# Three couples in the first chunk of a Strassen matmul, with VectorE's order and the results' sources moved

## The chip, the cores and the metric

The kernel runs on one core of one Trainium2 chip. Its time is device time in microseconds, the median over several executions. A profile is one execution in which a hardware profiler also records the instructions; its times are counted from the start of the span, which is a little shorter than the device time of that execution. A "slot" below is the time of sixteen 512-column matmuls on TensorE, the unit in which the kernel plans.

## The reference

```python
a: (4096, 4096) float32, b: (4096, 4096) float32, bias: (4096,) float32
out = np.tanh(np.matmul(a, b) + bias)
```

## The kernel before

The product is made in float16 with Strassen's scheme in Winograd's form: a block of the output is cut into four quarters and computed with seven products m1 to m7 instead of eight.

**Chunks and items.** The 4096 output columns are four chunks of 1024. In a chunk, 16 pairs of 128-row tiles are worked off. An *item* is such a pair with the chunk's columns: 256 rows by 1024 columns, seven products of 16 matmuls each (128x128 weights from a, 512 columns from b, contraction 2048). `PRODUCTS` names for each product its left operand (a quarter or a sum of quarters of a: a11, a12, a21, a22, s1, s2, s5, s6, s7) and its right operand (b11, b22, or sums d1, d3, d4, e6, e7 of quarters of b, kept in SBUF for the whole chunk). In the first chunk, three pairs are done in the opening in the plain way (lines 1459 and before), items 0 to 10 are single pairs, and items 11 and 12 do two pairs half and half, where chunks meet.

**Slots.** Everything is written out by hand in slots: `at_slot(slot, f, ...)` hangs work on a slot, and the loop at the end of the kernel goes through the slots, first runs the work hung there, then issues the products due, then the groups of the couples. An item n has the slots from 7n on; its products stand at positions 0 (m2), 2 (m5), 4 (m3), 5 (m1), 6 (m4), 8 (m6), 10 (m7), so that two items interleave. Each engine executes its queue strictly in the order in which this loop writes it: an instruction that waits holds up everything behind it on that engine.

**What is prepared for an item.** `prepare(n)` hangs up the loads of a (`load_nat`, GpSimd's queue, float32 to float16, sixteen of 128 KB per item, into tiles called `nat`), the turns (`turn`: VectorE transposes `nat` tiles into the quarters, line 281), the sums s1 to s7 (`asum`, VectorE, line 155), and `keep`, which stores the quarters in DRAM for the later chunks (SyncE's queue, line 311). The sums are made in place: s2 and then s6 over a21, s5 and then s7 over a12. The pool `wide` has eight tiles; an item's `nat` data take four of them. A load into such a tile waits until the turns that read it are through, and the quarters have two buffers each, so a turn waits until TensorE has read the same quarter of two items before (for a21 that is m6, which reads s6).

**After a product.** `after` takes sums and results. m2 and m5 share a bank: VectorE makes two sums with the bias from the bank after m2 (into the d bank and into `s`), and m5 then accumulates onto it, so it has to wait for both. After m3 ScalarE copies the bank to `cs`, after m4 to `ds`; `result` lets ScalarE make the tanh into a tile `o` of the pool `outs` (three tiles), and `store` writes it out (SyncE's queue, line 504). m1's sum writes into m3's bank, which becomes the bank of m6.

**Couples.** In two places of the first chunk two items are a *couple* (`ones`, set by `ONE_BASE` and `ONES`; the second item of a couple is in `behind_one`): their m3 are computed together with one more level of Strassen, seven products of eight matmuls at 256 columns instead of 32 at 512. The groups are issued at positions 4 (`group0`), 6 (`group1`), 8 (`single` 7 and 3 with m1, then `single` 4). They need four sums of a11 of both items (`left`, tiles `h`, two tiles of `wide` from `new_lefts` on until `end_ones`), three sums of d3 in tiles `one` and a fourth in place of a quarter of d3; that quarter is stored to DRAM before (`move`, SyncE) and brought back after the last couple (`end_ones`, GpSimd). `group1` and `twice_four` add an intermediate `x` to halves of the two items' banks; the last group writes into a half that the second of these adds reads.

In the trace, line 489 is `product`, line 794 is `multiply` (the groups of a couple), line 155 is every tensor_tensor of VectorE, line 281 the transposes, line 514 `result`, line 253 and 261 the loads, line 643 `move`. In row names a number behind a tile's name tells buffers apart.

Of the kernel before, what the change touches and what calls it, by code (L numbers as in the profile page):

```python
# [47 lines left out]

LEAD = 3
BEHIND = {"m7": 9}, {"m4": 3}  # L50
ONE_BASE, ONES = 6, 2
ONE_AT = {"m1": 8, "m4": 5, "m6": 10}
ONE_FROM = SLOTS * ONE_BASE - 1
FIRST = {0: 6, 2: 0, 4: 4, 5: 5, 6: 2, 8: 8, 10: 10}
# [70 lines left out]
def kernel(  # L125
# [391 lines left out]
    def after(n, s, what, st):  # L517
        c, pairs, part, _ = items[n]
        pair = pairs[s]
        first, last = part in (None, 0), part in (None, 1)  # L520
        if what == "m2":
            add21 = bias_bc[:, :NB] if first else asides[pair][0]
            add12 = bias_bc[:, NB:] if first else asides[pair][1]
            st["d"] = bank(n, s, "d")
            if n in second:
                st["ds"] = temps.tile([P, NB], fp32, name="ds", tag="ds")
                tt(st["ds"], st["z"], add21, ADD)
            else:
                tt(st["d"], st["z"], add21, ADD)
            st["s"] = temps.tile([P, NB], fp32, name="s", tag="sc")  # L530
            tt(st["s"], st["z"], add12, SUB)
        elif what == "m5":
            st["c"] = bank(n, s, "c")
            if n in twos or n in ones or n in behind_one:
                tt(st["s"], st["z"], st["s"], SUB)
                if n in second or n in behind_one:
                    twice_after(n, "m3")
            else:
                tt(st["c"], st["z"], st["s"], SUB)
        elif what == "m3":  # L540
            if last:
                st["cs"] = temps.tile([P, NB], fp32, name="cs", tag="sc")
                nc.scalar.copy(st["cs"], st["c"])
                if not first:
                    tt(st["cs"], st["cs"], asides[pair][2], ADD)
                result(st["c"], pair, 0, c, 1)
            else:
                asides[pair] = [
                    tl[:, i]
                    for tl in (wide.tile([P, 2, NB], fp32, name="aside", tag="wide") for _ in range(2))  # L550
                    for i in range(2)
                ]
                nc.scalar.copy(asides[pair][1], st["c"])
        elif what == "m1":
            if last:
                st["v"] = bank(n, s, "v")
                if n in partner or n in ones:
                    twice_four(n, "m3", 2)
                if n < len(items) - 1:
                    tt(st["v"], st["cs"], st["z"], SUB)  # L560
                else:
                    st["w"] = bank(n - 1, s, "z")
                    for to, half in ((st["v"], LAST[0]), (st["w"], LAST[1])):
                        tt(to[:, half], st["cs"][:, half], st["z"][:, half], SUB)
            else:
                st["v"] = bank(n, s, "v")
                nc.scalar.activation(st["v"], st["z"], COPY, scale=-1.0)
        elif what == "m4":
            if last:
                st["ds"] = temps.tile([P, NB], fp32, name="ds", tag="ds")  # L570
                nc.scalar.copy(st["ds"], st["d"])
                if not first:
                    tt(st["ds"], st["ds"], asides[pair][3], ADD)
                result(st["d"], pair, 1, c, 0)
            else:
                nc.scalar.copy(asides[pair][0], st["d"])
        elif what == "m6":
            if last:
                result(st["v"], pair, 1, c, 1)
            else:  # L580
                nc.scalar.copy(asides[pair][2], st["v"])
        else:
            if last:
                if n in twos and n + 2 < len(items) and not again(n + 2) and not natural(n + 2):
                    fetch(n + 2, "a12")
                o = new_out()
                tt(o, st["ds"], st["z"], SUB)
                nc.scalar.activation(o, o, TANH)
                store(o, pair, 0, c, 0)
            else:  # L590
                nc.scalar.activation(asides[pair][3], st["z"], COPY, scale=-1.0)
# [710 lines left out]
    def lead_after(n, what, st):  # L1302
        c, (pair,), part, _ = items[n]
        if what == "m2":
            st["c"] = bank(n, 0, "c")
            tt(st["c"], bias_bc[:, NB:], st["z"], SUB)
            if n:
                set_aside(st)
        elif what == "m3":
            st["cs"] = temps.tile([P, NB], fp32, name="cs", tag="sc")  # L1310
            nc.scalar.copy(st["cs"], st["c"])
            result(st["d"], pair, 1, c, 0)
        elif what == "m1":
            st["v"] = st["c"]
            tt(st["v"], st["cs"], st["w"], SUB)
        elif what == "m5":
            o = new_out()
            tt(o, st["cs"], st["z"], ADD)
            nc.scalar.activation(o, o, TANH)
            store(o, pair, 0, c, 1)  # L1320
            tt(st["ds"], st["ds"], st["z"], SUB)
        elif what == "m6":
            result(st["v"], pair, 1, c, 1)
        elif what == "m7":
            o = new_out()
            tt(o, st["ds"], st["w"], SUB)
            nc.scalar.activation(o, o, TANH)
            store(o, pair, 0, c, 0)

# [6 lines left out]
    def prepare(n):  # L1336
# [5 lines left out]
        elif natural(n):  # L1342
            loads = {0: (-5, -4), 1: (4, 5), 2: (6, 7)}.get(n, (s0 - 7, s0 - 4))
            for r in (1, 0):
                at_slot(loads[r if n in behind_one else 1 - r], load_nat, n, r)
                if n == 1 and r:
                    at_slot(loads[0], store_ends, "A")
            turns = {
# [4 lines left out]
            }.get(n, [(i, (s0 + x, s0 + y)) for i, (x, y) in {  # L1353
                "a22": (0, 0), "a21": (2, 2), "a11": (3, 4), "a12": (5, 5)
            }.items()])
            if n in behind_one:
                turns = [(i, (s0 + x, s0 + y)) for i, (x, y) in (
                    ("a11", (0, 1)), ("a22", (2, 2)), ("a21", (3, 3)), ("a12", (4, 5)),
                )]
            if n == 4 and n not in behind_one:  # L1360
                turns[0] = "a22", (s0 + 1, s0 + 1)
            if n - 3 in fours and part is not None:
                turns[0] = "a22", (s0 + 1, s0 + 2)
            if n - 2 in fours:
                turns = [("a22", (3, 3)), ("a21", (4, 4)), ("a11", (5, 8)), ("a12", (6, 8))]
                turns = [(i, (s0 + x, s0 + y)) for i, (x, y) in turns]
            for name, at in turns:
                at_slot(at[0], turn, n, name, 0)
            for name, at in turns:
                at_slot(at[1], turn, n, name, 1)  # L1370
                if n == 0 and name == "a22":
                    at_slot(-1, asum, n, "s2", 0)
                if name in ("a11", "a22") and not stays(n):
                    at_slot({0: {'a22': -1, 'a11': 5}, 1: {'a22': 12, 'a11': 15}, 2: {'a22': 17, 'a11': 18}}.get(n, {}).get(name, at[1]), keep, n, name)
        else:
            behind = n - 2 in partner
            for name, at in (
                ("a22", 1 if behind else 0), ("a21", 1),
                ("a11", -1 if n in second else 0 if behind else 2), ("a12", 4),
            ):  # L1380
                if part == 1 and n - 2 in fours and name != "a12":
                    continue
                if name == "a12" and n - 2 not in twos and n > LEAD + 1 and n - 2 not in fours:
                    early_fetch.add(n)
                elif name != "a12" or n - 2 not in twos:
                    at_slot(s0 + at, fetch, n, name)
# [17 lines left out]
        if natural(n) and n - 2 in fours:  # L1404
            sums_at["s2"], sums_at["s5"] = 5, 8
        if n in ones:
            sums_at.update(s1=14, s6=15, s7=15)
        if n - 2 in twos and n not in twos and part is None:
            sums_at["s5"] = 8
        for name, at in sums_at.items():  # L1410
# [386 lines left out]
```

## Time and profile before

| | |
|---|---|
| runs shown | 1502.38, 1502.63, 1508.91 us |
| median | 1502.63 us |
| profiled execution | 1501.84 us, span 1499.9 us |
| TensorE clock granted, mean | 0.999 |
| TensorE busy | 1492.3 us of the span |
| VectorE, ScalarE, GpSimd busy | 1226.1, 404.1, 528.5 us |
| first chunk's items | from about 90 us to about 400 us |
| couples of the first chunk | m3's first group at 244.65 and at 292.85 us |

The profile's rows are to be read so: start in us, length in us, engine, line, operation, written tile <- read tiles, shapes, count; in brackets the idle time of the engine before the row and what ended it. Lists of waits give engine and line that waited, what it waited for, total us, number of times, longest. PE is TensorE, DVE VectorE, ACT ScalarE, POOL GpSimd, SPq SyncE's DMA queue. Rows that begin with a stretch such as 260.00:270.00 give busy us (and instructions) of TensorE's matmuls, its weight loads, VectorE, ScalarE and GpSimd, then the granted clock, the busy share of the DMA engines and GB/s. The length of a matmul row is modelled, so the pace is read from the starts.

### The profile page before, as it was taken

How to read it: one execution, taken by the hardware profiler on the slowest of the kernel's cores; microseconds unless marked ns; L12 is line 12 of the kernel's file. 1: busy time of each engine (PE TensorE's matmuls, PEld its weight loads, DVE VectorE, ACT ScalarE, POOL GpSimd, SP SyncE). 2: the span in 40 equal slices, each digit the busy share in tenths (PEclk: the TensorE clock that was granted, in tenths of full speed). 3: DMA queues.
4: the chain of work that ended last, by engine and by line, in shares of the span. 5: the costliest groups of instructions: out<-in, count | busy, mean ns of one | idle time of the engine just before them, and what ended most of it. 6: DMA issues, size and time to landing. Idle time of an engine off the chain costs nothing.

```text
span 1499.9 us, 25071 instructions
## 1 busy us (share of the span) xinstructions
PE 1492.3 (99%) x9509; PEld 927.9 (62%) x9509; DVE 1226.1 (82%) x1742; ACT 404.1 (27%) x915; POOL 528.5 (35%) x925
## 2 busy tenths in 40 slices
PE   9999999999999999999999999999999999999998
PEld 4444445444445788864444578888644468888886
DVE  6788979887787888967888788889658869888887
ACT  4431111111222233321122223333222222333332
POOL 8775454354523111245751321111434121111112
PEclk9999999999999999999999999999999999999999
DMA  9999999799999799889999988998998687888895
GB/s 186 184 244 266 298 268 271 188 256 204 185 343 306 258 326 342 314 308 260 191 286 323 288 287 311 329 341 311 318 280 213 221 286 269 299 321 300 324 339 184
DMA packets 211132, 413.51 MB, mean 276 GB/s; under 512 B 26178, under 2 KB 102466, under 8 KB 211012
## 3 DMA queue, kind: packets, MB, share of 16 engines
q0 software_dynamic: 124992, 220.00, 59.2%
q1 hardware_dynamic: 85348, 191.53, 36.4%
q8 instruction: 74, 1.21, 0.3%
q10 hardware_dynamic: 672, 0.39, 0.1%
q14 instruction: 46, 0.38, 0.1%
HBM read 352.33 MB, written 138.94 MB: 328 GB/s over the span
## 4 chain that ended last, share of the span: by engine, by line
PE 93%; DMA 4%; DVE 2%; issue 0%; POOL 0%; ACT 0%; DVEq 0%; POOLq 0%
PE ps L489 42%; PE ps L794 37%; PE ps L858 9%; PE ps L1459 6%; DMA nat<-in_a_dram 3%; DVE a L281 1%; DVE a L155 1%; DMA coarse<-in_a_dram 0%; DVE s L155 0%; DVE h L155 0%; POOL nat L261 0%; DVE ps L155 0%; POOL nat L253 0%; PE warm L1519 0%; PE spread L452 0%
## 5 line engine op out<-in xcount | busy, mean ns | idle before, releaser
L489 PEld LDWEIGHTS <-a 128*128 128x128 f16 x2592 | 253.0, 98 | 303.2 <-issue 0.9
L794 PEld LDWEIGHTS <-h 128*128 128x128 f16 x3008 | 293.6, 98 | 37.6
L730 POOL DMA_DIRECT2D form<-form_m x196 | 103.9, 530 | 537.0 <-PE ps L794 485.2
L794 PEld LDWEIGHTS <-a 128*128 128x128 f16 x2256 | 220.1, 98 | 36.5 <-issue 1.4
L489 PE MATMUL ps<-b,a 128*128 128x512 f16 x868 | 198.2, 379 | 0.4 <-DVE s L155 0.4
L489 PE MATMUL ps<-d,a 128*128 128x512 f16 x800 | 180.3, 379 | 0.0
L281 DVE STREAM_TRANSPOSE a<-nat 128x1024 f16<-128x1024 f16 (+3 forms) x178 | 155.8, 917 | 19.9 <-PE ps L489 15.3
L155 DVE TENSOR_TENSOR a<-a,a 128x2048 f16<-128x2048 f16 (+1 forms) x135 | 162.5, 1206 | 0.2
L489 PE MATMUL ps<-e,a 128*128 128x512 f16 x700 | 158.7, 379 | 0.0
L794 PE MATMUL ps<-form,h 128*128 128x256 f16 x1136 | 144.7, 273 | 0.0
L155 DVE TENSOR_TENSOR h<-a,h 128x1024 f16<-128x1024 f16 x188 | 127.9, 687 | 15.8 <-PE ps L794 15.7
L391 POOL DMA_DIRECT2D b<-in_b_dram x208 | 112.0, 543 | 74.7 <-PE ps L489 33.4
L794 PE MATMUL ps<-form,a 128*128 128x256 f16 x896 | 111.5, 273 | 0.2
L253 POOL DMA_DIRECT2D nat<-in_a_dram x144 | 76.5, 535 | 93.3 <-DMA nat<-in_a_dram 48.0
L858 PE MATMUL ps<-d,a 128*128 128x512 f16 x480 | 108.2, 379 | 0.0
L489 PEld LDWEIGHTS <-s 128*128 128x128 f16 x624 | 60.9, 98 | 72.4
L880 ACT CAST ps<-zeros 128x256 f32<-128x256 f16 x196 | 70.1, 380 | 127.7 <-DVE s L155 68.9
L858 PEld LDWEIGHTS <-a 128*128 128x128 f16 x608 | 59.4, 98 | 65.9
L489 PE MATMUL ps<-d,s 128*128 128x512 f16 x432 | 97.6, 379 | 0.0
L155 DVE TENSOR_TENSOR ds<-ds,ps 128x512 f32<-128x512 f32 (+1 forms) x126 | 83.5, 674 | 9.2 <-PE ps L858 8.3
L155 DVE TENSOR_TENSOR ps<-ps,x 128x256 f32<-128x256 f32 x100 | 43.0, 430 | 47.4 <-PE ps L794 37.2
L794 PE MATMUL ps<-d,a 128*128 128x256 f16 x608 | 78.8, 273 | 0.0
(173 smaller groups left out, 1950.3 us busy)
## 6 DMA issues: line engine op xcount, KB each, us to landing
form<-form_m POOLq DMA_DIRECT2D x196, 512.0 KB, 7.2
a<-scratch SPq DMA_DIRECT2D x148, 512.0 KB, 7.3
out_dram<-o SPq DMA_DIRECT2D x186, 256.0 KB, 6.0
nat<-in_a_dram POOLq DMA_DIRECT2D x256, 128.0 KB, 7.8
scratch<-a SPq DMA_DIRECT2D x48, 512.0 KB, 8.3
b<-in_b_dram POOLq DMA_DIRECT2D x176, 128.0 KB, 5.6
form_m<-stage POOLq DMA_DIRECT2D x18, 512.0 KB, 6.5
scratch<-a SPq DMA_DIRECT2D x32, 256.0 KB, 8.1
```

Of the source, the lines that this page charges most:

```text
L155: nc.vector.tensor_tensor(out=out_, in0=in0, in1=in1, op=op)
L253: nc.gpsimd.dma_start(out=tl[ds(q * QP, QP), :, :], in_=src.rearrange("(mb p) k -> p mb k", p=QP),)
L281: nc.vector.transpose(dst[:, ds(b0 * tb, n * tb), :].rearrange("P (b t) (mb p) -> P mb b t p", t=tb, p=QP), src[:, :, ds(b0, n), :].rearra ...
L391: nc.gpsimd.dma_start(out=dst[ds(q * QP, QP), ds(t, nt)], in_=src)
L489: nc.tensor.matmul(st[where], at, bt, start=(what == "m2" or n < LEAD and what == "m1") and i == 0, stop=i == len(ts_) - 1, skip_group_che ...
L730: nc.gpsimd.dma_start(out=rights[what, name], in_=forms[what, name])
L794: nc.tensor.matmul(to, at, bt, start=False, stop=t == TP - 1, skip_group_check=True)
L858: nc.tensor.matmul(to[:, half], at[:, t // TB, t % TB], bop[right, t // TB][:, t % TB, half], start=anew and t == 0, stop=t == T - 1, skip ...
L880: nc.scalar.copy(bank(n, 0, where)[:, HALF[half]], zeros)
L1459: nc.tensor.matmul(mb[m % 4, j], aq[m, kt // T][:, kt % T, :], right(kt, j), start=fresh and kt == k0, stop=stop and kt == k1 - 1, skip_gr ...
```

## The change

Four things change, all in the first chunk except where `after` serves a few single items of later chunks:

- `ONE_BASE, ONES = 5, 3`: the couples are items (5, 6), (7, 8), (9, 10) instead of (6, 7), (8, 9). The sums of d3 are made seven slots earlier, its quarter is stored seven slots earlier (slot 20 instead of 27), and brought back seven slots later (72 instead of 65).
- s6 and s7 of a couple's first item are hung on the slot after the one that holds the couple's third step (16 instead of 15, counted from seven slots before the item).
- The turn of a22 of every item of the first chunk from item 4 on, other than the second of a couple, stands a slot later, behind the sums of m2. Before, only item 4 had this.
- The tanh of m3 and m4 reads ScalarE's copy instead of the bank, and m7's sum and tanh are made in place in `ds` instead of a tile of `outs`.

```diff
-ONE_BASE, ONES = 6, 2
+ONE_BASE, ONES = 5, 3
...
-                result(st["c"], pair, 0, c, 1)
+                result(st["cs"] if first else st["c"], pair, 0, c, 1)
...
-                result(st["d"], pair, 1, c, 0)
+                result(st["ds"] if first else st["d"], pair, 1, c, 0)
...
-                o = new_out()
+                o = st["ds"] if c == 0 and part is None else new_out()
                 tt(o, st["ds"], st["z"], SUB)
...
-            o = new_out()
-            tt(o, st["ds"], st["w"], SUB)
+            o = st["ds"]
+            tt(o, o, st["w"], SUB)
...
-            if n == 4 and n not in behind_one:
+            if n >= 4 and items[n][0] == 0 and n not in behind_one:
                 turns[0] = "a22", (s0 + 1, s0 + 1)
...
         if n in ones:
-            sums_at.update(s1=14, s6=15, s7=15)
+            sums_at.update(s1=14, s6=16, s7=16)
```

What that makes of VectorE's queue in the first couple, from its second-last step on. Before (items 6 and 7; a22_2254 is a22 of item 8, the sums over a21_1919 and a12_2004 are s6 and s7 of item 6, x_2250 the intermediate):

```order
L155 TENSOR_TENSOR a11_1942<-a22_1865,a11_1942 128x2048
L281 STREAM_TRANSPOSE a22_2254<-nat_2056 128x2x16x32
L281 STREAM_TRANSPOSE a22_2254<-nat_2061 128x2x16x32
L155 TENSOR_TENSOR ps_0_247<-ps_7_254,bias_bc_109 128x512
L155 TENSOR_TENSOR s_2286<-ps_7_254,bias_bc_109 128x512
L155 TENSOR_TENSOR a21_1919<-a21_1919,a11_1942 128x2048
L155 TENSOR_TENSOR a12_2004<-a11_1942,a12_2004 128x2048
L155 TENSOR_TENSOR ps_2_249<-ps_2_249,x_2250 128x256
L155 TENSOR_TENSOR s_2090<-ps_5_252,s_2090 128x512
L155 TENSOR_TENSOR ps_5_252<-s_2090,ps_4_251 128x512
```

After, VectorE at the same place of its first couple (items 5 and 6; a22_2091 is a22 of item 7, the sums over a21_1736 and a12_1817 are s6 and s7 of item 5):

```order
L155 TENSOR_TENSOR a11_1759<-a22_1711,a11_1759 128x2048
L155 TENSOR_TENSOR ps_6_253<-ps_4_251,bias_bc_109 128x512
L155 TENSOR_TENSOR s_2089<-ps_4_251,bias_bc_109 128x512
L281 STREAM_TRANSPOSE a22_2091<-nat_1867 128x2x16x32
L281 STREAM_TRANSPOSE a22_2091<-nat_1872 128x2x16x32
L155 TENSOR_TENSOR ps_5_252<-ps_5_252,x_2056 128x256
L155 TENSOR_TENSOR s_1899<-ps_2_249,s_1899 128x512
L155 TENSOR_TENSOR ps_2_249<-s_1899,ps_7_254 128x512
L155 TENSOR_TENSOR a21_1736<-a21_1736,a11_1759 128x2048
L155 TENSOR_TENSOR a12_1817<-a11_1759,a12_1817 128x2048
```

The two sums of m2 (those that read `bias_bc`) now stand ahead of the turn of a22, and s6 and s7 behind the add of `x` and the two sums of m3 and m1.

The second place is where the item after the last couple begins, again on VectorE. Before (a22_2864 is a22 of item 11; the sums with `bias_bc` follow m2 of item 10):

```order
L155 TENSOR_TENSOR ps_2_249<-s_2683,ps_7_254 128x512
L155 TENSOR_TENSOR a12_2583<-a11_2470,a12_2583 128x2048
L155 TENSOR_TENSOR a12_2820<-a12_2820,a11_2763 128x2048
L281 STREAM_TRANSPOSE a22_2864<-nat_2656 128x4x8x32
L281 STREAM_TRANSPOSE a22_2864<-nat_2661 128x4x8x32
L155 TENSOR_TENSOR ps_6_253<-ps_4_251,bias_bc_109 128x512
L155 TENSOR_TENSOR s_2894<-ps_4_251,bias_bc_109 128x512
L155 TENSOR_TENSOR s1_2915<-a22_2652,a11_2763 128x2048
```

After (the item that follows the last couple is item 11, whose two pairs need two such sums each; a22_3104 is a22 of item 12):

```order
L155 TENSOR_TENSOR ps_5_252<-s_2882,ps_4_251 128x512
L155 TENSOR_TENSOR a12_2786<-a11_2674,a12_2786 128x2048
L155 TENSOR_TENSOR a12_3029<-a12_3029,a11_2965 128x2048
L155 TENSOR_TENSOR ps_6_253<-ps_7_254,bias_bc_109 128x512
L155 TENSOR_TENSOR s_3099<-ps_7_254,bias_bc_109 128x512
L155 TENSOR_TENSOR ps_0_247<-ps_3_250,bias_bc_109 128x512
L155 TENSOR_TENSOR s_3102<-ps_3_250,bias_bc_109 128x512
L281 STREAM_TRANSPOSE a22_3104<-nat_2855 128x4x8x32
L281 STREAM_TRANSPOSE a22_3104<-nat_2860 128x4x8x32
```

The turn of a22 moved behind the sums of m2 here too.

The third place is GpSimd's queue of loads at the end of the chunk. Before (d3's quarter comes back behind the first loads of item 11):

```order
L261 DMA nat_2656<-in_a_dram 32x4x512 x4
L261 DMA nat_2661<-in_a_dram 32x4x512 x4
L643 DMA d3_0_495<-away_m3_0_t3_1661 128x4x256
L643 DMA d3_1_592<-away_m3_0_t3_1661 128x4x256
L261 DMA nat_2766<-in_a_dram 32x4x512 x4
L261 DMA nat_2771<-in_a_dram 32x4x512 x4
```

After:

```order
L261 DMA nat_2754<-in_a_dram 32x4x512 x4
L261 DMA nat_2759<-in_a_dram 32x4x512 x4
L261 DMA nat_2855<-in_a_dram 32x4x512 x4
L261 DMA nat_2860<-in_a_dram 32x4x512 x4
L643 DMA d3_0_495<-away_m3_0_t3_1478 128x4x256
L643 DMA d3_1_592<-away_m3_0_t3_1478 128x4x256
L261 DMA nat_2968<-in_a_dram 32x4x512 x4
L261 DMA nat_2973<-in_a_dram 32x4x512 x4
```

The two loads of d3 moved behind sixteen more loads of a, and stand ahead of the last eight.

## The prediction

> **What bounds the kernel now.** I read the page first, then the waits of TensorE alone, then the chain of waits, and last the timelines of TensorE, VectorE, GpSimd and SyncE from 150 to 400 us, where the first chunk's couples lie.
>
> ```profile
> span 1499.9 us, 25071 instructions
> PE 1492.3 (99%) x9509; PEld 927.9 (62%) x9509; DVE 1226.1 (82%) x1742; ACT 404.1 (27%) x915; POOL 528.5 (35%) x925
> PE 93%; DMA 4%; DVE 2%; issue 0%; POOL 0%; ACT 0%; DVEq 0%; POOLq 0%
> ```
> ```profile
> PE warm L1519 <- DVE idle L427: 1.3, 1, 1.3
> PE tp L1560 <- DVE first L1555: 0.6, 1, 0.6
> PE ps L794 <- DVE ps L155: 0.5, 1, 0.5
> PE ps L489 <- DVE s L155: 0.4, 1, 0.4
> ```
>
> TensorE is busy for 99% of the span, and after the opening it waits for another engine just twice in the whole program, both times for VectorE. So there are two things to win or lose: matmul time, and waits of TensorE in the stretch that the change touches. The chain of waits gives the rate of each kind of matmul, from long unbroken runs (start, length, count):
>
> ```profile
> 578.99 34.97 PE ps L794 x320
> 685.21 141.59 PE ps L489 x656
> ```
>
> A 256-column matmul takes 34.97/320 = 0.1093 us, a 512-column one 141.59/656 = 0.2158 us.
>
> **The third couple.** A couple replaces m3 of two items (2 x 16 matmuls of 512 columns, 32 x 0.2158 = 6.91 us) by seven groups of eight at 256 columns (56 x 0.1093 = 6.12 us). One couple more removes 0.79 us from TensorE, which has nothing to hide it behind.
>
> **The first wait.** The last group of the first couple (line 794, reading `one`) overwrites a half bank that VectorE's add of `x` still reads.
>
> ```profile
> 258.51 1.91 PE L794 MATMUL ps<-d,h 128*128 128x256 f16 x16
> 260.90 1.03 PE L794 MATMUL ps<-one,a 128*128 128x256 f16 x8 [0.48 <-DVE ps L155]
> 265.22 1.03 PE L489 MATMUL ps<-side,a 128*128 128x512 f16 x4
> ```
> ```profile
> 254.69 2.37 DVE L281 STREAM_TRANSPOSE a<-nat 128x1024 f16<-128x1024 f16 x2
> 256.99 0.67 DVE L155 TENSOR_TENSOR ps<-ps,bias_bc 128x512 f32<-128x512 f32 x1
> 257.56 0.67 DVE L155 TENSOR_TENSOR s<-ps,bias_bc 128x512 f32<-128x512 f32 x1
> 258.16 2.34 DVE L155 TENSOR_TENSOR a<-a,a 128x2048 f16<-128x2048 f16 x2
> 260.42 0.42 DVE L155 TENSOR_TENSOR ps<-ps,x 128x256 f32<-128x256 f32 x1
> ```
>
> The sixteen matmuls before it end at 258.51 + 16 x 0.1093 = 260.26, so the group is 0.64 us late: 0.48 idle, the rest is the restart of the pipeline. VectorE was late because s6 and s7 (258.16, 2.26 us up to the next start) stood ahead of the add. The change puts both behind it. VectorE is then free at 258.16, the add can run once its eight matmuls are through (258.51 + 0.87 = 259.38), and ends near 260.0. The wait goes: -0.64 us. What becomes late next is s6: after the add come two 0.6 us sums that need the group's end (to about 261.7), then s6 (to 262.8) and s7 (to 263.9). m6, which reads s6, starts at 265.22 - 0.64 = 264.58. Margin 1.8 us; VectorE has idle time after s7 (below), so nothing behind is pushed. The second couple of before had the add just in time, so a wait has nothing to lose there either.
>
> **The second wait.** It stands where item 10, uncoupled before, follows the last couple: m5 accumulates in the bank that the two sums of m2 read.
>
> ```profile
> 326.66 1.03 PE L489 MATMUL ps<-side,a 128*128 128x512 f16 x4
> 334.16 3.61 PE L489 MATMUL ps<-b,a 128*128 128x512 f16 x16 [0.43 <-DVE s L155]
> ```
> ```profile
> 316.50 2.49 DVE L281 STREAM_TRANSPOSE a<-nat 128x256 f16<-128x256 f16 x4 [5.30 <-PE ps L489]
> ...
> 328.31 2.34 DVE L155 TENSOR_TENSOR a<-a,a 128x2048 f16<-128x2048 f16 x2
> 330.57 2.37 DVE L281 STREAM_TRANSPOSE a<-nat 128x1024 f16<-128x1024 f16 x2
> 332.86 0.67 DVE L155 TENSOR_TENSOR ps<-ps,bias_bc 128x512 f32<-128x512 f32 x1
> 333.43 0.68 DVE L155 TENSOR_TENSOR s<-ps,bias_bc 128x512 f32<-128x512 f32 x1
> ```
>
> m2 and m6 from 326.66 on are 32 matmuls: m5 was due at 333.57 and came at 334.16, 0.59 us late. VectorE had stood still for 5.30 us until TensorE let go of a buffer, then worked without a gap, and the a22 turn (330.57, 2.29 us) stood ahead of the sums. With the turn a slot later the sums start at 330.57 instead of 332.86 and end at about 331.8, 1.8 us ahead of m5. -0.59 us. Between two couples half a turn of a11 (1.2 us) still stands ahead of the sums; before has this too, and it was in time there:
>
> ```profile
> 284.75 0.67 DVE L155 TENSOR_TENSOR s<-ps,bias_bc 128x512 f32<-128x512 f32 x1
> ```
> ```profile
> 285.94 3.62 PE L489 MATMUL ps<-b,a 128*128 128x512 f16 x16
> ```
>
> It ends at 285.35 for a start at 285.94: 0.6 us of margin, at two places now instead of one. I cost the shift at nothing on that cover; were a load late there, the price is its lateness less 0.6.
>
> **The third couple's work on VectorE.** Four `h` sums and two adds of `x`, and a sum in place of ScalarE's copy of each m3: 4 x 0.65 (row at 293.00, below) + 2 x 0.42 + 2 x 0.68 = 4.8 us more for the two items. Cover: the idle 5.30 us quoted above, in which s6 and s7 (2.26 us) now run too. By the new order VectorE still stands some 3.0 us idle at that turn in each couple, so lateness of one couple isn't handed to the next. If that cover were gone, each us of it would be a us of TensorE.
>
> **The loads.** Two of the eight `wide` tiles hold the `h` operands in couples, from slot 35 instead of 42, so the loads have three pairs of tiles for one more item pair. A pair of loads waits for the a21 turn that frees its tile:
>
> ```profile
> 273.40 4.25 POOL L253 DMA_DIRECT2D nat<-in_a_dram  x8 [16.83 <-DVE s L155]
> ```
> ```profile
> 288.86 1.25 DVE L281 STREAM_TRANSPOSE a<-nat 128x1024 f16<-128x1024 f16 x1 [1.11 <-DMA nat<-in_a_dram]
> ...
> 293.00 0.65 DVE L155 TENSOR_TENSOR h<-a 128x1024 f16<-128x1024 f16 x1
> ```
> ```profile
> 293.72 1.04 PE L794 MATMUL ps<-one,h 128*128 128x256 f16 x8
> ```
> ```profile
> DMA to landing us min/median/max: 4.8/8.4/11.5
> ```
>
> The last of the eight issues ended at 277.65, its data was there at 288.86, VectorE was 1.11 us behind, and `h` was ready at about 293.6 for matmuls at 293.72. That is the tightest place: 0.15 us. In the new order the same chain (m6 ends, a21 turns, tile free, load, a22 turn, a21 turn, `h`) stands twice, at couples two and three, at the same distance from its m6. Bounds: below, nothing, since before did it in time; above, 1.1 us each, the wait seen here once again. I take nothing, the value of the very chain, and keep 2 x 1.1 for the range.
>
> **Queues.** SyncE's two stores of d3's quarter and GpSimd's two loads of it back only move: the stores a whole item earlier, the loads one item later and past sixteen more `nat` loads.
>
> ```profile
> 182.67 1.09 SPq L643 DMA_DIRECT2D away_m_t<-d  x2
> ```
> ```profile
> 311.75 1.54 POOL L643 DMA_DIRECT2D d<-away_m_t  x2 [0.62 <-issue]
> ```
> ```profile
> 341.06 3.62 PE L489 MATMUL ps<-d,a 128*128 128x512 f16 x16
> ```
> ```profile
> DVE a L281 <- DMA nat<-in_a_dram: 2.6, 2, 1.5
> ```
>
> The first m3 that reads the quarter comes 29 us after the issue; both move by the same seven slots. The `nat` loads that now stand behind it are held up by 1.54 us of issue and are first read seven slots (24 us) later. The stores push SyncE's later ones by 1.09 us and take DMA time 24 us sooner; between 90 and 400 us VectorE waited only twice for a load (2.6 us in all) and TensorE never, so a load later by a us there stops nobody. Nothing for all of it.
>
> **The results.** tanh of m3 and m4 reads ScalarE's copy, m7's result stays in `ds`, and the ring of three result tiles takes three tiles an item instead of four. ScalarE did wait for that ring:
>
> ```profile
> 202.74 0.60 ACT L514 ACTIVATE o<-ps 128x512 f32<-128x512 f32 x1 [2.19 <-DMA out_dram<-o]
> ```
>
> But no wait of TensorE goes back to ScalarE in the waits above, and it is busy for 27%. Between 0 and nothing measurable; I take 0. `ds` has two tiles, and the next writer of the same tile is m4 two items on, nine slots (31 us) after m7: no new wait.
>
> **Sum.** -0.79 - 0.64 - 0.59 = -2.02 us on the profiled execution of 1501.84 us: 1499.8. The median of the runs shown is 0.79 above that execution, so 1500.6.
>
> **Rivals.**
> 1. The waits move rather than go: TensorE waits up to 1.1 us for `h` at couples two and three because the loads land later. For it: the 0.15 us. Against: the longest landing in this stretch, 11.5 us, is hardly above what happened here, and the chain is no longer than before. Time: 1500.6 + 2.2 = 1502.8.
> 2. The waits stay and only the couple's 0.79 counts: 1501.8. For it: VectorE is nearly full in this stretch. Against: what stood ahead of the late sums is now behind them.
> 3. Slower: the loads don't keep up with three buffer pairs. It decides from the point where a load is more than about 3 us late, because then VectorE's idle time no longer absorbs it and each couple and item 11 pass it on. With 3 us lost at each of three couples: 1500.6 + 9 = 1509.6. Against: one single wait of VectorE for a load, of 1.11 us, in both couples of before.
> 4. Faster by more: excluded by the waits of TensorE; there is no more than what I took.
>
> How long a wait matters for the clock too. In the two windows that hold the waits the granted clock is 1.00:
>
> ```profile
> 260.00:270.00 10.00, 9.52 (x51) 4.73 (x50) 4.38 (x7) 0.63 (x1) 0.00 (x0) 1.00 0.39 108
> 330.00:340.00 10.00, 9.57 (x46) 4.20 (x44) 9.77 (x13) 0.60 (x1) 3.80 (x7) 1.00 1.14 294
> ```
>
> The Trainium skill, "TensorE: Matmul & The Clock Gate", section "Part 1: The HAM clock gate", says that the array falls back to half clock after about 3.4 us of idleness and needs about as long to come back. By that rule my sum stays as it is, and rival 3 would be an estimated 1.7 us dearer for each wait beyond 3.4 us; no wait here is long enough to show it.
>
> **How the numbers follow.** My case 0.60, around 1499.5 to 1501.5; rivals 1 and 2 together 0.28, up to 1503.6; rival 3 0.08; the rest 0.04 for what I don't see, split between both signs. The range 1499.3 to 1503.8 holds my case and rivals 1 and 2. A change of 0.5% is 7.5 us, about what a measurement of this kernel tells from none: my case and rivals 1 and 2 lie within it (0.89), rival 3 beyond (0.09 with its part of the rest), faster 0.02.
>
> **What would show it.** Right: half as many matmuls again that read `one`; no row of TensorE waiting for VectorE after 100 us; m2 of item 11 about 2.0 us earlier than before's, relative to the span's start. Wrong: a wait of TensorE for `h` at a couple's second group, for a sum of m2 ahead of m5, or VectorE waiting several us for `nat` loads.

## The result and the profile after

The changed kernel takes 1500.78 us (median of 16 runs, 1499.68 to 1504.83), the kernel before 1502.91 us (16 runs, 1501.71 to 1508.91). The ratio is 0.9981, 95% interval 0.9974 to 0.9987: 2.1 us, where 2.02 was forecast. The profiled execution after took 1500.06 us, the one before 1501.84.

The page of the changed kernel, its first lines and TensorE's share of the chain of waits; then all waits of TensorE for other engines (engine, line, what it waited for, total us, times, longest):

```profile
span 1498.2 us, 25123 instructions
PE 1491.5 (100%) x9533; PEld 932.7 (62%) x9533; DVE 1229.7 (82%) x1750; ACT 406.8 (27%) x918; POOL 528.6 (35%) x925
PE 98%; DMA 1%; DVE 1%; issue 0%; ACT 0%; DVEq 0%
```
```profile
PE warm L1519 <- DVE idle L427: 1.3, 1, 1.3
PE tp L1560 <- DVE first L1555: 0.5, 1, 0.5
PE ps L794 <- DVE ps L155: 0.4, 1, 0.4
```

Both waits of before are gone from the first chunk. The one of 0.4 us that is left stands in the third chunk, at 908.59 us, outside the stretch that the prediction is about. The chain of waits gives the accounts (start, length, count). Of before, the first plain product, the stretch behind the second wait, the first groups of the second chunk, and the place in the third chunk:

```profile
9.99 79.43 PE ps L1459 x368
334.16 124.48 PE ps L489 x576
458.64 1.75 PE ps L794 x16
910.24 28.14 PE ps L794 x256
```

The same places of after:

```profile
10.20 79.43 PE ps L1459 x368
332.44 124.32 PE ps L489 x576
456.75 1.75 PE ps L794 x16
908.59 28.14 PE ps L794 x256
```

From the first plain product to the second chunk it is 448.65 us before (458.64 - 9.99) and 446.55 after: -2.10, where the sum had -2.02. The three remaining differences lie outside that stretch: the first plain product began 0.21 us later, the second chunk ran 0.11 shorter (-1.89 at its start, -2.00 at the long run of groups at 578.99 before and 576.99 after), and the third ran 0.35 longer up to 908.59. With them the span is 1.7 us shorter.

### The profile page after: what moved, and what is told of

The parts are those of the page before. It is cut to its first block, busy times and chain, and to the rows that moved or that the text cites. A ratio compares the mean times of both kernels' runs of the same rounds, so it can differ in the third digit from the quotient of the medians.

```text
span 1498.2 us, 25123 instructions
## 1 busy us (share of the span) xinstructions
PE 1491.5 (100%) x9533; PEld 932.7 (62%) x9533; DVE 1229.7 (82%) x1750; ACT 406.8 (27%) x918; POOL 528.6 (35%) x925
## 3 DMA queue, kind: packets, MB, share of 16 engines
q8 instruction: 75, 1.23, 0.3%
## 4 chain that ended last, share of the span: by engine, by line
PE 98%; DMA 1%; DVE 1%; issue 0%; ACT 0%; DVEq 0%
PE ps L489 46%; PE ps L794 38%; PE ps L858 8%; PE ps L1459 6%; DMA out_dram<-o 1%; DMA coarse<-in_a_dram 0%; DVE h L155 0%; PE warm L1519 0%; DVE ps L155 0%; DVE ds L155 0%; PE tp L1560 0%; PE spread L452 0%; DVE s L155 0%; DVE e L155 0%; DVE a L155 0%
## 5 line engine op out<-in xcount | busy, mean ns | idle before, releaser
L794 PEld LDWEIGHTS <-h 128*128 128x128 f16 x3040 | 297.4, 98 | 37.5
L155 DVE TENSOR_TENSOR a<-a,a 128x2048 f16<-128x2048 f16 (+1 forms) x141 | 169.3, 1206 | 0.2
L281 DVE STREAM_TRANSPOSE a<-nat 128x1024 f16<-128x1024 f16 (+3 forms) x178 | 155.7, 917 | 13.8 <-PE ps L489 8.9
L489 PEld LDWEIGHTS <-s 128*128 128x128 f16 x592 | 57.9, 98 | 68.6
L155 DVE TENSOR_TENSOR ds<-ds,ps 128x512 f32<-128x512 f32 (+1 forms) x137 | 90.7, 673 | 9.2 <-PE ps L858 8.3
L489 PE MATMUL ps<-d,s 128*128 128x512 f16 x400 | 90.4, 379 | 0.0
```

Of the source, the lines that this page charges most:

```text
L155: nc.vector.tensor_tensor(out=out_, in0=in0, in1=in1, op=op)
L281: nc.vector.transpose(dst[:, ds(b0 * tb, n * tb), :].rearrange("P (b t) (mb p) -> P mb b t p", t=tb, p=QP), src[:, :, ds(b0, n), :].rearra ...
L489: nc.tensor.matmul(st[where], at, bt, start=(what == "m2" or n < LEAD and what == "m1") and i == 0, stop=i == len(ts_) - 1, skip_group_che ...
L794: nc.tensor.matmul(to, at, bt, start=False, stop=t == TP - 1, skip_group_check=True)
```

## The experiments

Two stretches are read from every trace: from the first plain product to m3 of item 2 (the opening), and from there to the first line 794 product of the second chunk (the items that the change touches).

| kernel | opening, us | items, us | median, us (ratio to the kernel before, run beside it) |
|---|---|---|---|
| before | 138.13 | 310.52 | 1502.91 |
| changed | 138.13 | 308.42 | 1500.78 (0.9981) |
| slots_alone | 139.55 | 309.21 | 1501.97 (0.9989) |
| couple_alone | 139.93 | 313.57 | 1507.54 (1.0030) |
| results_alone | 139.05 | 310.47 | 1503.25 (0.9999) |
| results_back | 139.05 | 309.71 | 1502.66 (0.9997) |
| couple_store27 | 138.56 | 309.79 | 1502.39 (0.9996) |
| tanh_only | 138.65 | 308.42 | 1501.44 (0.9992) |
| a22_back | 139.27 | 309.01 | 1501.96 (0.9992) |
| vec_20 | 138.13 | 314.09 | 1506.87 (1.0024) |
| vec_48 | 138.54 | 352.27 | 1544.75 (1.0277) |
| four_couples | 141.93 | 315.16 | 1511.54 (1.0055) |
| ends_early | 142.81 | 308.42 | 1501.90 (0.9993) |
| four_ends | 141.02 | 323.42 | 1514.99 (1.0077) |

The medians are uncertain by about 0.1%, so the verdicts below rest on the second stretch, of one profile each; where TensorE waits for nothing in it, it repeats to 0.01 us (changed, tanh_only, ends_early). The first four expectations name the sum of both stretches; they were split afterwards, because the first varies by up to 1.8 us among kernels that are nearly alike up to there. In results_back the chain of waits puts 0.63 us of it down to loads of `nat`.

### One part at a time

The order of VectorE alone:

```diff
 ONE_BASE, ONES = 6, 2
-            if n == 4 and n not in behind_one:
+            if n >= 4 and items[n][0] == 0 and n not in behind_one:
-            sums_at.update(s1=14, s6=15, s7=15)
+            sums_at.update(s1=14, s6=16, s7=16)
```

> The kernel before with the moves in VectorE's order alone (s6 and s7 of a couple's first item at 16, the turn of a22 a slot later), two couples as before. The measure is the stretch from TensorE's first plain product to its first L794 product of the second chunk: 448.65 us in before, 446.55 in the changed kernel. My theory: both waits of TensorE for VectorE (0.64 and 0.59 us late) go and nothing takes their place, the stretch is 447.4 and the median 1.2 us below before. Rival, the waits move: a wait of 0.4 us or more stands elsewhere between 200 and 420 us, the stretch is above 448.

309.21 us, 1.31 less than before (forecast 1.23), and no wait of TensorE between 150 and 420 us. Both waits went and did not move. The whole stretch that the expectation names gained nothing in this profile (448.76 us), since its opening took 1.42 us longer, 0.44 of that a wait at 149.29 us.

The third couple alone:

```diff
-ONE_BASE, ONES = 6, 2
+ONE_BASE, ONES = 5, 3
```

> The kernel before with three couples from item 5 on, VectorE's order as before. My theory: the couple's 0.79 us comes off whole; the add of x that stands behind s6 and s7, and the sums of m2 behind the turn of a22, are late where they were late in before: 448.65 - 0.79 = 447.86. Rival 1: with less idle time on VectorE the old order is late at each of the three couples (0.64 each): 449.1, no faster than before. Rival 2: the loads do not keep up, VectorE waits over 3 us for nat tiles and the stretch is over 450.

None of the three: 313.57 us, 3.05 *more* than before. The whole stretch is above 450 as in rival 2, but VectorE's longest wait for a load is 2.2 us. TensorE's waits in the first chunk (start, length, bracket: idle before, and for whom):

```profile
149.97 3.61 PE L489 MATMUL ps<-d,a 128*128 128x512 f16 x16 [1.63 <-DVE ps L155]
189.45 1.02 PE L489 MATMUL ps<-side,a 128*128 128x512 f16 x4 [1.33 <-DVE ps L155]
195.17 3.61 PE L489 MATMUL ps<-b,a 128*128 128x512 f16 x16 [2.10 <-DVE s L155]
242.50 1.03 PE L794 MATMUL ps<-one,a 128*128 128x256 f16 x8 [0.49 <-DVE ps L155]
363.39 3.61 PE L489 MATMUL ps<-b,a 128*128 128x512 f16 x16 [0.43 <-DVE s L155]
```

The first is the opening's, the last two are the two waits of before. The two at 189 and 195 us are new, and they lie 37 us ahead of the first couple's first group (226.25 us), where neither the groups nor their sums have begun.

The results' sources alone, and the changed kernel without them:

```diff
-                result(st["c"], pair, 0, c, 1)
+                result(st["cs"] if first else st["c"], pair, 0, c, 1)
-                result(st["d"], pair, 1, c, 0)
+                result(st["ds"] if first else st["d"], pair, 1, c, 0)
-                o = new_out()
+                o = st["ds"] if c == 0 and part is None else new_out()
-            o = new_out()
-            tt(o, st["ds"], st["w"], SUB)
+            o = st["ds"]
+            tt(o, o, st["w"], SUB)
```

> The kernel before with the results' sources alone (tanh of m3 and m4 from ScalarE's copy, m7 in place in ds). My theory: ScalarE's waits for the ring of result tiles go in the first chunk, TensorE's time does not change: stretch 448.65 +- 0.1, both waits of TensorE still there (0.48 and 0.43 idle). Rival: ScalarE held TensorE up unseen, the stretch is shorter by 0.3 us or more. On the wait of 0.39 us at 908.59 that the changed kernel has in the third chunk and before has not: if it is the ring of result tiles that now turns with another phase, it is here too; if it is only a store that landed late in that execution, it comes or not by chance.

310.47 against 310.52: nothing, as forecast.

> The changed kernel with the results' sources as before. My theory: the results are worth nothing, stretch 446.55 +- 0.1, no wait of TensorE between 200 and 420 us. Rival: three couples need the result tiles or banks sooner, TensorE waits for ScalarE or for a sum behind it, 0.3 us or more, and the stretch is over 446.9. The wait at 908.59: gone if the ring's phase is its cause, by chance otherwise.

309.71 us, 1.29 above the changed kernel: the rival. So the same edit is worth nothing in the kernel before and 1.3 us in the changed one. In results_back the chain of waits runs through it (start, length, what; the pieces of 0.02 to 0.04 us between these are left out):

```profile
164.51 22.34 DMA out_dram<-o
186.93 0.61 ACT o L514
187.56 0.71 DVE ps L155
188.31 11.82 PE ps L489 x54
```

A result store issued at 164.51 us lands after 22.34 us. ScalarE's tanh of m3 waits for its tile; VectorE's m1 sum, which overwrites the bank that this tanh reads, waits for ScalarE; TensorE's m6 waits for that sum. In results_back the waits of these three, from the timelines of ScalarE, VectorE and TensorE:

```profile
186.93 0.60 ACT L514 ACTIVATE o<-ps 128x512 f32<-128x512 f32 x1 [9.48 <-DMA out_dram<-o]
187.56 0.70 DVE L155 TENSOR_TENSOR ps<-cs,ps 128x512 f32<-128x512 f32 x1 [7.71 <-ACT o L514]
188.31 1.02 PE L489 MATMUL ps<-side,a 128*128 128x512 f16 x4 [1.12 <-DVE ps L155]
```

And just ahead of the late store on SyncE's queue stands the store of d3's quarter (`away`), which the third couple brought to slot 20:

```profile
162.47 0.32 SPq L311 DMA_DIRECT2D scratch<-a  x1
162.84 1.57 SPq L643 DMA_DIRECT2D away_m_t<-d  x2
164.51 6.38 SPq L504 DMA_DIRECT2D out_dram<-o  x1
170.99 1.49 SPq L311 DMA_DIRECT2D scratch<-a  x1
```

Is it that store, or the couple's other work? And which half of the results' edit covers it?

### The store of d3, and what hides it

```diff
-ONE_BASE, ONES = 6, 2
+ONE_BASE, ONES = 5, 3
-    at_slot(ONE_FROM - 14, move, "m3", 0, True)
+    at_slot(ONE_FROM - 7, move, "m3", 0, True)
```

> Three couples alone, as in couple_alone, but the quarter of d3 is stored at slot 27 as in before instead of slot 20. The measure from here on leaves out the opening: from m3 of item 2 (about 148 us) to the first L794 product of the second chunk: 310.52 us in before, 308.42 in the changed kernel, 313.57 in couple_alone. Theory: the earlier store of d3 falls among the stores of a's quarters, the result stored behind it lands after 22 us, ScalarE waits 9.7 us for its ring, VectorE 7.9 us behind ScalarE, TensorE 1.33 and 2.10 us behind VectorE. With the store at slot 27 these waits are gone and the couple's 0.79 counts: 309.7. Rival 1: it is not the store but VectorE's and the loads' extra work for a couple that begins an item sooner: the two waits stay, 313 or more. Rival 2: the waits come back seven slots later, behind the store at slot 27, in the couple itself: 311 or more.

309.79 us for a forecast of 309.7; only the two waits of before are left (0.48 and 0.43 us). With nothing else changed than the slot of two stores, 3.78 us are gone against couple_alone. The store's place is the cause, and the couple itself is worth 310.52 - 309.79 = 0.73 us.

How much the late store costs hangs on VectorE's order too. results_back is couple_alone with the new order and nothing else, and its items are 3.86 us shorter (313.57 - 309.71), where the same order is worth 1.31 in the kernel before. In couple_alone the late VectorE still does the turn of a22 (191.58 us, 2.36 long) ahead of the sums of m2, and TensorE waits 2.10 us for these; in results_back the sums come first, at 190.44, and that wait is gone.

The changed kernel with the last four lines of the results' edit undone, the tanh of m3 and m4 left as changed:

```diff
-                o = st["ds"] if c == 0 and part is None else new_out()
+                o = new_out()
-            o = st["ds"]
-            tt(o, o, st["w"], SUB)
+            o = new_out()
+            tt(o, st["ds"], st["w"], SUB)
```

> The changed kernel, but m7's result in tiles of the ring again; the tanh of m3 and m4 still reads ScalarE's copies. Theory: what the new results are worth is that VectorE's sum into m3's bank no longer waits for a tanh that waits for a tile of the ring: 308.42 as in the changed kernel, no wait of TensorE near 188 us, though ScalarE still waits 9 us for the ring. Rival: it is the fourth tile of the ring an item that matters, ScalarE's copies of m3 and m4 stand behind the late tanh in its queue, so VectorE still waits some 7 us for a copy and TensorE about 1.1 us: 309.7, as in results_back.

308.42 us, that of the changed kernel to the hundredth. ScalarE waits even longer for its tile, but VectorE's sum doesn't:

```profile
187.51 0.63 ACT L514 ACTIVATE o<-cs 128x512 f32<-128x512 f32 x1 [10.43 <-DMA out_dram<-o]
```
```profile
180.01 0.70 DVE L155 TENSOR_TENSOR ps<-cs,ps 128x512 f32<-128x512 f32 x1 [0.53 <-PE ps L489]
```

So it is the source of the tanh that matters: it takes the late store off the path to TensorE by releasing the bank. The ring's fourth tile an item doesn't show in TensorE's time.

### VectorE's cover

The changed kernel with the turn of a22 in its old slot:

```diff
-            if n >= 4 and items[n][0] == 0 and n not in behind_one:
+            if n == 4 and n not in behind_one:
```

> The changed kernel with the turn of a22 back in its old slot (but for item 4). Theory: only the second wait comes back, where the item after the last couple begins: 308.42 + 0.59 = 309.0 from m3 of item 2 to the second chunk, the first wait (ahead of the reader of one) stays away since s6 and s7 are at 16. Rival: with the couples close together every turn of a22 holds up the sums of m2, a wait of 0.4 us or more at each couple: 310 or more; or none, since the item after the last couple is now one of two pairs: 308.42.

309.01: the second wait alone is back, 0.59 us, at the item after the last couple (0.43 idle before 358.26). Between couples nothing is held up.

48 extra multiplications on VectorE for each couple. They were hung on the slot of s7, and came behind the turn of a21 instead of ahead of it:

```diff
+    for n in ones:
+        for _ in range(48):
+            at_slot(SLOTS * n + 9, tt, ident, ident, ident, MUL)
```

> The changed kernel with 48 idle multiplications of a 128x128 f16 tile by itself on VectorE behind s7 of each couple, where it stands still for 2.96 us until m6 lets go of a21; the results do not use that tile. By the prediction's sentence (each us beyond the cover is a us of TensorE) with the slack seen in the trace: if the 48 take D us, TensorE waits D - 2.96 - 0.55 at the m5 that follows the sums of m2 (0.55 is how far these sums are ahead of m5 at 260.8 and 261.34). From the rows for 1024 and 2048 elements I estimate D at 5.2, so 1.7 us at each of three couples: 308.42 + 5.1 = 313.5. Rival: later gaps of VectorE take it up (0.72 us before the sum at 264.99 and 1.2 us at 278.85), TensorE waits less than 0.5 us in all and the stretch is under 309.

352.27. My estimate of their length was far off (12.4 us, 0.257 each, for 128 elements a partition, where 1024 take 0.65), and they delayed two sums for which TensorE waits at once. So it doesn't measure the cover, but it shows a late VectorE going through whole: 12.06 us at each couple, and more behind it, since the 32 matmuls that follow take 9 to 10 us instead of 7.07:

```profile
247.06 12.41 DVE L155 TENSOR_TENSOR ident<-ident 128x128 f16<-128x128 f16 x48
259.38 1.41 DVE L155 TENSOR_TENSOR s<-ps,s 128x512 f32<-128x512 f32 x2
```
```profile
260.12 9.98 PE L489 MATMUL ps<-d,a 128*128 128x512 f16 x32 [12.06 <-DVE s L155]
322.80 9.37 PE L489 MATMUL ps<-d,a 128*128 128x512 f16 x32 [12.06 <-DVE s L155]
384.86 9.05 PE L489 MATMUL ps<-d,a 128*128 128x512 f16 x32 [12.05 <-DVE s L155]
```

Twenty of them in the place that was meant:

```diff
+        if n in ones:
+            late_ones = [(s0 + 16, tt, ident, ident, ident, MUL)] * 20
...
+        for at in late_ones:
+            at_slot(*at)
```

> The changed kernel with 20 idle multiplications by themselves on VectorE (0.257 us each in vec_48, 5.1 us) behind s7 of each couple and ahead of the turn of a21, so in the place where VectorE stands still for 2.96 us. In vec_48 they stood behind that turn, ahead of two sums that TensorE waits for at once. Theory: the idle time covers 2.96 us, what is over (2.2 us, less 0.1 to 0.2 of slack at the sums behind the turn) is waited for by TensorE at each of the three couples: about 2.1 us each, 446.55 + 6.5 = 453 from the first plain product to the second chunk's first L794 product. No wait is above 3.4 us, so the clock stays at 1.00. Rival 1: the cover is none, since the turn waits for m6 anyway and the sums behind it are late by all of it: 3 x 5.1 = 15 us, 462. Rival 2: it is absorbed, under 447.5.

314.09, 5.67 more than the changed kernel: 1.89 a couple, for 2.1 forecast. VectorE's idle time at this place in the changed kernel, and what stands there now:

```profile
244.27 2.49 DVE L281 STREAM_TRANSPOSE a<-nat 128x256 f16<-128x256 f16 x4 [2.96 <-PE ps L489]
291.82 2.49 DVE L281 STREAM_TRANSPOSE a<-nat 128x256 f16<-128x256 f16 x4 [2.96 <-PE ps L489]
339.38 2.49 DVE L281 STREAM_TRANSPOSE a<-nat 128x512 f16<-128x512 f16 x4 [2.96 <-PE ps L489]
```
```profile
240.07 5.16 DVE L155 TENSOR_TENSOR ident<-ident 128x128 f16<-128x128 f16 x20
```
```profile
249.40 7.07 PE L489 MATMUL ps<-d,a 128*128 128x512 f16 x32 [1.73 <-DVE s L155]
```

The extra work holds VectorE for 5.08 us (240.07 to 245.15); 2.96 are covered, of the other 2.12 TensorE pays 1.89. The cover is real and ends where the idle time ends.

### A fourth couple

```diff
-ONE_BASE, ONES = 5, 3
+ONE_BASE, ONES = 3, 4
```

> The changed kernel with four couples, from item 3 to item 10, all else by the same rules (the quarter of d3 is stored at slot 6). Theory, the couple's price again: 308.42 - 0.79 = 307.63 if nothing new is late. Rival 1: the store of d3 at slot 6 meets the stores of the opening's results and of a's quarters, some result lands after 20 us or more, ScalarE and VectorE wait for it and TensorE waits 1 us or more in the stretch of 100 to 200 us: 309 or more. Rival 2: items 3 and 4 have their loads only just in time (VectorE waited 1.77 us for one at 145.78 in the changed kernel), with the first couple's sums on top TensorE waits 3 us or more.

Slower than before, by 0.55% (0.42 to 0.68%). TensorE waits twice, at items 2 and 3, and the 16 matmuls behind each wait take 5.30 us, not 3.62:

```profile
152.12 5.30 PE L489 MATMUL ps<-d,a 128*128 128x512 f16 x16 [3.54 <-DVE ps L155]
175.24 5.30 PE L489 MATMUL ps<-b,a 128*128 128x512 f16 x16 [4.00 <-DVE s L155]
```

The chain of waits ahead of the second goes from load to load of `nat`, but its last step leads from a load straight to m5, which reads no `nat` tile. VectorE's own rows ahead of the two waits say more:

```profile
150.24 1.25 DVE L281 STREAM_TRANSPOSE a<-nat 128x1024 f16<-128x1024 f16 x1 [1.50 <-DMA nat<-in_a_dram]
171.51 1.30 DVE L281 STREAM_TRANSPOSE a<-nat 128x256 f16<-128x256 f16 x2 [2.44 <-DMA scratch<-a]
172.74 1.25 DVE L155 TENSOR_TENSOR one<-one,d 128x1024 f16<-128x1024 f16 x2
```

The first wait goes back to loads, rival 2. Ahead of the second, VectorE waits for a store of a quarter of a (`keep`), whose tile the turn overwrites, and then makes two sums for the couple before those of m2. Neither rival names that wait.

The stores of `ends`, whose tiles those loads take, moved from GpSimd's queue at slot 7 to SyncE's at slot 1, first in the changed kernel and then with four couples (there with the store of d3 at slot 13):

```diff
-    def store_ends(g):
+    def store_ends(g, queue=nc.gpsimd):
...
-                nc.gpsimd.dma_start(
+                queue.dma_start(
...
-        (0, store_ends, "B"), (7, store_ends, "C"),
+        (0, store_ends, "B"), (1, store_ends, "C", nc.sync),
```

> The changed kernel with the four stores of the tiles ends (results of the opening, ready at 86.7 us) issued by SyncE at slot 1 in place of GpSimd at slot 7 (119.5 us). In results_back the chain of waits runs from these stores over the loads of item 2 to a wait of TensorE of 0.63 us at 149 us; waits of 0.2 to 1.6 us stand there in six of the ten profiles. Theory: the stores hold the tiles that those loads need; freed 30 us sooner the loads come in time always, 138.1 us from the first plain product to m3 of item 2 (138.13 in the changed kernel), and the median falls by 0.3 to 0.5 us. Rival: it is the DMA engines' load, not the tiles; the stores only move into a full stretch, the wait stays by chance, or results of the opening land later.

No gain, as in the rival: the median is 1501.90 us. The items keep their 308.42 us. The opening takes 4.7 us longer in the profile, which here is the slowest of the eleven executions (1500.44 to 1504.84 us), so it shows what can happen and not the usual run: TensorE waits earlier (1.21 us at 114.44, 1.45 at 128.15) for VectorE, which waits for loads that landed late there. From 90 to 150 us the DMA engines are as full with one as with the other (busy us and instructions of the five engines, clock, DMA share, GB/s; the changed kernel, then this one):

```profile
90.00:150.00 60.00, 60.00 (x280) 27.20 (x278) 53.56 (x61) 13.13 (x24) 34.33 (x64) 1.00 1.11 272
```
```profile
90.00:150.00 60.00, 57.04 (x264) 25.49 (x263) 53.41 (x61) 13.33 (x25) 32.38 (x60) 1.00 1.11 267
```

> Four couples, with the quarter of d3 stored at slot 13 instead of 6 and the stores of ends by SyncE at slot 1. In four_couples TensorE waited 3.54 us at 152 and 4.00 us at 175 and ran behind each at half clock for a while (16 matmuls in 5.30 us), 457.1 from the first plain product to the second chunk. Theory: the loads of items 2 and 3 were late by the tiles of wide and by the store of d3 that went out with them; now the waits are gone or under 1 us and the stretch is 445.8 to 447. Rival: VectorE and the loads have no room for a couple's work at items 3 and 4 whatever the stores do: the two waits stay, 455 or more.

The rival's number, 464.44 us in the whole stretch, but not its reason, that the stores make no difference. TensorE waits for VectorE at items 2 and 3, and ahead of both waits VectorE waits for stores of a's quarters:

```profile
167.54 1.02 PE L489 MATMUL ps<-side,a 128*128 128x512 f16 x4 [3.25 <-DVE ps L155]
180.57 6.42 PE L489 MATMUL ps<-b,a 128*128 128x512 f16 x16 [9.42 <-DVE s L155]
```
```profile
161.02 2.49 DVE L281 STREAM_TRANSPOSE a<-nat 128x256 f16<-128x256 f16 x4 [6.26 <-DMA scratch<-a]
176.84 1.30 DVE L281 STREAM_TRANSPOSE a<-nat 128x256 f16<-128x256 f16 x2 [4.70 <-DMA scratch<-a]
```

These stores, on SyncE's queue too, land after 16.9 us in the median between 130 and 180 us, against 9.5 in four_couples. So by these rows both waits here end with late stores and not with late loads. Which of the moved stores delays them was not tried, and whether a fourth couple would pay with the stores placed otherwise is open. No version tried is faster than the changed kernel. The changed kernel with d3's store at slot 27 was not run; TensorE waits for nothing in its items, so no gain is left there.

## Why the prediction was right, and where it was not

- **The sum.** -2.02 forecast, -2.10 measured between the first plain product and the second chunk, -2.13 in the medians.
- **The third couple**, 0.79: 0.73 in couple_store27.
- **The first wait**, 0.64: slots_alone gives 1.31 for both waits, a22_back 0.59 for the second, so 0.72 is left for the first.
- **The second wait**, 0.59: 0.59.
- **VectorE's cover.** "some 3.0 us idle at that turn in each couple": 2.96 three times. "Each us of it would be a us of TensorE": 1.89 of 2.12, over a couple.
- **The tightest place.** I gave `h` 0.15 us at couples two and three, and rival 1 rested on it. In the profile after, VectorE waits for no load there, and `h` is ready 0.47 us ahead of its matmuls (268.65 to 269.12):

```profile
268.00 0.65 DVE L155 TENSOR_TENSOR h<-a 128x1024 f16<-128x1024 f16 x1
```
```profile
269.12 1.04 PE L794 MATMUL ps<-one,h 128*128 128x256 f16 x8
```

The 1.11 us by which a load was late in before came back at none of the three couples, so in the changed kernel that chain does not set `h`.
- **Wrong: the step "Queues", "Nothing for all of it".** I had SyncE's later stores 1.09 us later, and asked who waits for the moved stores and for the loads, but not who waits for what is stored *behind* them. By itself, the earlier store costs 3.78 us (couple_alone against couple_store27): the result behind it lands 22 us after its issue, and the tile that it holds is what ScalarE needs next. I had the row that points there, ScalarE's wait of 2.19 us for the same ring, and put it aside because it cost TensorE nothing in that kernel.
- **Wrong: the step "The results", "I take 0".** Its reason, that no wait of TensorE goes back to ScalarE, held for the kernel before (results_alone: nothing). In the changed kernel the edit is worth 1.29 us, just because it takes the late store off TensorE's path. The two errors cancel, since both edits are in the change: without the second it brings 0.81 us in the items instead of 2.10 (results_back), and the third couple by itself loses 3.05. VectorE's new order, counted in the sum for its two waits only, takes a part of that loss too. Taken one at a time the three parts give -1.31 + 3.05 - 0.05 = +1.69 us in the items; together they give -2.10. That the sum came out so close is in part luck: its terms are right, but that nothing else would cost anything held only because the parts cover one another.
- **Rival 3** came true for one couple more, 10.5 us over the changed kernel in the two stretches together, but by its mechanism only in part: loads are behind the first wait of four_couples, stores of a's quarters ahead of the second and of both in four_ends.
- **What a measurement tells.** I took a change of 0.5% for about the least that a measurement shows. The interval of this one is 0.0013 wide, so even a change of 0.19% can be told from no change.
- **Not settled:** the wait at 908.59 us in the third chunk, a miss by the sign "no row of TensorE waiting for VectorE after 100 us". It stands behind VectorE's wait of 1.00 us for a result store, and came in five of the fourteen profiles (0.35 to 0.56 us), with the old results (couple_alone, couple_store27) and with the new, and its cause wasn't looked for. Nor was it tried which of the transfers ahead of it, or the issue itself (6.38 us), makes the result store at 164.51 us land after 22 us.

## What to carry to other kernels

An edit that is worth nothing alone can be what makes another one pay: cost parts of a change together wherever one fills a queue and another releases what waits behind it, or puts urgent work ahead of what can wait. For every transfer that is moved, ask not only who waits for it, but whose buffers are held by the transfers queued behind it, and follow that through each in-order engine to the one that sets the end. And before adding work to a busy engine, measure its idle time at the very place: here 2.96 us of idle time took up 2.96 of 5.08 us of extra work, and the rest was paid nearly in full.

## What the runs showed of the hardware

- The clock of TensorE. In four_ends it ran on at full speed after a wait of 3.25 us (granted clock 1.00), in four_couples it fell after waits of 3.54 and 4.00 (the stretches behind these waits, with the granted clock third from the right; four_ends first):

```profile
168.00:172.00 4.00, 3.15 (x15) 1.34 (x14) 4.00 (x6) 1.40 (x3) 1.76 (x4) 1.00 1.08 304
```
```profile
152.00:156.00 4.00, 3.88 (x11) 1.50 (x11) 3.96 (x7) 0.59 (x1) 3.54 (x7) 0.58 1.08 257
175.00:179.00 4.00, 3.76 (x12) 1.45 (x12) 4.00 (x7) 0.00 (x0) 1.85 (x4) 0.69 1.10 273
```

  Sixteen matmuls then took 5.30 us instead of 3.62, so such a wait costs 1.68 us beyond itself. The Trainium skill, "TensorE: Matmul & The Clock Gate", section "Part 1: The HAM clock gate", puts the limit at about 3.4 us. These rows agree, and the 1.7 us that the prediction estimated from it fits these two waits. It is too little for the longer ones: behind 9.42 us in four_ends sixteen matmuls took 6.42 us (2.80 more), behind 12.06 in vec_48 thirty-two took 2.0 to 2.9 us more.
- A store of 256 KB can take 22.3 us to land where the median of the result stores from 150 to 200 us is 13.8 (results_back), and that is long enough to reach TensorE over ScalarE and VectorE.
- A VectorE multiplication of 128 elements a partition, in place and in a row with others, takes 0.257 us (vec_48), over a third of the 0.65 us that a sum of 1024 takes.
